# A two-group attention layer: another queue and earlier places for the copies that begin the precomputed weight sums

## The chip, the cores and the metric

The kernel runs on one core of one Trainium2 chip. The metric is the device time of one execution in microseconds (us), the median of several runs. An execution has five engines with a program each: PE (matrix multiply; its weight loads are shown as PEld), DVE, ACT and POOL (elementwise work), and SP, which here only issues DMA transfers. ACT and POOL can issue DMA transfers too. All transfers share the core's 16 DMA engines.

## What is computed

One layer of a hybrid encoder for 1024 new positions ("prompt") and 32 further ones with a cache of 512. After a combined input projection come two attentions, A (top-k sparse, softmax) and B (stick-breaking), two gated branches, and a feed-forward network. Only its end is needed here:

```python
m = jax.nn.sigmoid(gate_a) * pa + jax.nn.sigmoid(gate_b) * pb
h = x + jnp.einsum('bld,de->ble', m, w_out)
u = jnp.einsum('bld,df->blf', rmsnorm(h, g_ffn), w_up)
return h + jnp.einsum('blf,fd->bld', jnp.square(jax.nn.relu(u)), w_down)
```

Sizes: model width 1024, feed-forward width 4096, 8 heads of 64 in each attention, all in float32. The matrix w_up is 1024 x 4096, 16 MB.

## The kernel before

**Tiles and stages.** The 1056 positions are columns. Weights come in units of [128, 512] float32 (256 KB): `unit` loads one from HBM to the tile `wst` (3 buffers), ACT rounds it into `wh` and POOL (sometimes DVE) takes the rest into `wl` (5 buffers each), and each product is then three matmuls (`wh` by `xh`, `wh` by `xl`, `wl` by `xh`). The stages in order of time: indexer and projections of mixer B; top-k and projections of mixer A (line 616, up to about 480 us); the early half of both attentions with gate projections between them (`attend`, lines 635 to 641, about 480 to 700 us); gates, branches and output of group 1, which is columns 0 to 511; the feed-forward network of group 1 (`ffn_group`, about 880 to 1320 us), with the late half of the attentions (the generator `late`, line 634) set between its units up to about 1137 us; then branches, output and feed-forward of group 2, the other 544 columns (`ffn_quads`).

`ffn_group` runs over 8 blocks `q`. A block has four `go_up(f)` (two units of w_up each, 24 matmuls of 128x512) and eight `go_down(e, q)` (one unit of w_down each, 12 matmuls). At the end it reloads 2 MB of `h` (`reload`, tile `xh<-dh`) and scales the output (`late_scale` and others, tile `y`).

**Weight sums.** Group 2 multiplies blocks of w_up with a scheme of seven products instead of eight (Strassen and Winograd). For it four sums of the four blocks w11, w12, w21, w22 are needed for each quarter of w_up: s1 = w21 + w22, s2 = s1 + w11, s3 = w11 + w21, s4 = s2 + w12. The generator `weight_sums` (line 430) makes them in HBM without any compute engine: a plain HBM-to-HBM copy of 1 MB begins a sum (`begin`, issued by SP), and a DMA that adds 1 MB to what is there ends it (`add`, issued by POOL, the only engine here that issues adding DMAs). 4 quarters x 4 sums make 16 copies and 16 adds. Their results, named `dw_up` in the profile, are read from about 1335 us on, as units of group 2.

**What sets the order.** All instructions are recorded by a planner (class `Plan`): `record` notes an instruction with its rank and its dependencies, and a list scheduler picks, engine by engine, the ready instruction of the best rank by a model of costs, in which all transfers go through one pipe (line 407). All are issued from line 410, so every row of the profile shows L410. Ranks run from FAST (0) to SLOW (4); a SLOW instruction goes only where its engine has nothing better that is ready in the model. `behind()` makes instructions depend, in the model only, on the last one recorded before; line 332 applies that to SP's alone. The order that comes out is fixed in the program; on the chip each engine takes its rows one after another and waits at semaphores. A step of `weight_sums` is taken at each `tick()` (line 459). The ticks stand in `ffn_group` at `go_up(f)` for f from 12 on and at `go_down(3, q)` for q from 3 on, 25 places for 24 steps.

**Semaphores of transfers.** The transfers that SP and ACT issue take turns on eight completion counters (DMAHW0 to DMAHW7 in the rows below), those of POOL on eight others (DMASW). A transfer waits until an earlier one on its counter has landed.

Of the kernel before, what the change touches and what calls it, by code (L numbers as in the profile page):

```python
# [14 lines left out]
ALU = mybir.AluOpType  # L15
# [37 lines left out]
FAST, PREP, MAIN, FILL, SLOW = 0, 1, 2, 3, 4  # L53
# [44 lines left out]
PE, DVE, ACT, POOL, SP = range(5)  # L98
# [4 lines left out]
class Plan:  # L103
# [175 lines left out]
    def record(self, eng, fn, op, args, kw):  # L279
        args = list(args)  # L280
        out = kw["out"] if "out" in kw else args[0]
        outs = [out] + ([kw["accum_out"]] if kw.get("accum_out") is not None else [])
        rest = args[1:] if "out" not in kw else args
        ins = [x for x in rest if isinstance(x, bass.AP)]
        ins += [x for k, x in kw.items() if isinstance(x, bass.AP) and k not in ("out", "accum_out")]
        reads = list(ins)
        if op == "copy_predicated":
            reads.append(out)
        n = Node()
        n.id, n.eng, n.call = len(self.nodes), eng, (fn, args, kw)  # L290
        n.key = (self.level[-1], n.id)
        n.occ, n.lat = self.cost(eng, op, out, ins, args[2] if op == "scalar_tensor_tensor" else None, kw)
        n.size = 0
        n.table = TABLE.get(args[2]) if op == "activation" else None
        n.store = op == "dma_start" and out.tensor.name not in self.onchip and self.level[-1] != FAST
        if op == "dma_start":
            n.size = 4
            for s in max((out, ins[0]), key=lambda z: z.size()).shape:
                n.size *= s
        n.lock = eng == POOL or eng == DVE and self.locks(op, out, ins, args)  # L300
        n.row = out.tensor.name if eng == PE and self.level[-1] == FILL else None
        n.wait = self.patience
        n.succ, n.need, n.ready, n.end, n.start = [], 0, 0.0, None, None
        self.nodes.append(n)
        deps = set()
        found = []
        for aps, write in ((reads, False), (outs, True)):
            for ap in aps:
                c = self.cells(ap)
                if c is None:  # L310
                    continue
                m, part, idx = c
                w = m.writer[part, idx]
                if (w < 0).any():
                    deps.update(m.old)
                    n.ready = max(n.ready, m.floor)
                deps.update(np.unique(w).tolist())
                if write:
                    for r, rpart, ridx in m.readers:
                        if rpart.start < part.stop and part.start < rpart.stop and self.meet(idx, ridx, m.writer.shape[1]):  # L320
                            deps.add(r)
                found.append((m, part, idx, write))
        for m, part, idx, write in found:
            if write:
                m.writer[part, idx] = n.id
                if m.writer.shape == (1, 1):
                    m.readers = []
            else:
                m.readers.append((n.id, part, idx))
            if not m.touched or m.touched[-1] != n.id:  # L330
                m.touched.append(n.id)
        if eng == SP and self.hold is not None:
            deps.add(self.hold)
        deps.discard(-1)
        deps.discard(n.id)
        for d in deps:
            d = self.nodes[d]
            if d.end is not None:
                n.ready = max(n.ready, self.after(d, n))
            else:  # L340
                d.succ.append(n)
                n.need += 1
        if not n.need:
            heapq.heappush(self.later[eng], (n.ready, n.id))
# [74 lines left out]
class Layer:  # L419
# [10 lines left out]
    def weight_sums(self):  # L430

        nc, a = self.nc, self.a
        for (w, q), s in self.sums.items():
            w11, w12, w21, w22 = (a[w][i, 4 * q:4 * q + 4].rearrange("t (a b) c -> (t a) (b c)", b=4) for i in range(4))
            s1, s2, s3, s4 = s

            def begin(out, src):
                with nc.behind():
                    nc.sync.dma_start(out, src)

            def add(out, src):
                nc.gpsimd.dma_start(out, src, accum_op=ALU.add, max_dma_last_dim=8192)

            begin(s1, w21)
            begin(s3, w11)
            yield
            add(s1, w22)
            add(s3, w21)
            yield
            begin(s2, s1)  # L450
            yield
            add(s2, w11)
            yield
            begin(s4, s2)
            yield
            add(s4, w12)
            yield

    def tick(self):

        with self.nc.rank(SLOW):
            next(self.steps, None)

    def split(self, h, l, x):
# [66 lines left out]
    def run(self):  # L531
        nc, a = self.nc, self.a
# [82 lines left out]
        self.rope_tables()  # L615
        for p in range(4):
            self.project_a(p)
        with nc.rank(SLOW):
            self.top_k()
        for e in GATES:  # L620
# [13 lines left out]
        late = (None for is_a in (False, True) for h in range(H) for _ in self.attend(h, is_a, (4, 6)))  # L634
        for is_a in (False, True):
            for h in range(H):
                for _ in self.attend(h, is_a, (0, 2)):
                    pass
                for _ in range(AHEAD if is_a and h == H - 2 else 0):
                    next(late)  # L640
                if h in NEWS:
                    self.attend_new(NEWS.index(h), is_a)
# [1019 lines left out]
    def ffn_group(self, g, late=iter(())):  # L1662
        nc, a = self.nc, self.a
        nq, us = DFF // 512, {}

        def source(name, row, col, t):

            return a[name][2 * row + col, t]

        def go_up(f):  # L1670
            units = [self.unit(source("w_up", f % 8 // 4, j, 4 * (f // 8) + f % 4)) for j in range(2)]
            us[f] = uh, ul = g.mh[:, f % 8], g.ml[:, f % 8]

            def done(c, cs, ps):
                r = g.tmp("ru", "pb", 3)
                nc.scalar.activation(r, ps, AF.Relu)
                nc.gpsimd.tensor_mul(r, r, r)
                nc.scalar.copy(uh[:, cs], r)
                nc.vector.tensor_sub(ul[:, cs], r, uh.bitcast(F32)[:, cs])

            self.column_block(units, lambda k, cs: (g.h[:, k, cs], g.l[:, k, cs]), done, g.chunks)

        def go_down(e, q):
            units = [self.unit(source("w_down", e % 2, q % 2, 4 * (q // 2) + e // 2))]

            def done(c, cs, ps):
                y = g.y[:, e, cs]
                if q == 0:
                    nc.scalar.copy(y, ps)
                elif q < nq - 1:  # L1690
                    nc.vector.tensor_add(y, ps, y)
                elif e < KB // 2:
                    self.late_scale(g, e, c, cs, ps)
                else:
                    self.finish(g, e, c, cs, ps)

            if q == nq - 1 and e >= KB // 2:
                for c, cs in enumerate(g.chunks):
                    self.early_scale(g, e, c, cs)
            self.column_block(units, lambda k, cs: (us[4 * q + k][0][:, cs], us[4 * q + k][1][:, cs]), done, g.chunks,  # L1700
                              kn=4)

        done = 0

        def beside(n):

            nonlocal done
            done += n
            while done >= PACE:
                done -= PACE  # L1710
                nc.patience = WAIT[2]
                with nc.behind():
                    next(late, None)
                nc.patience = WAIT[1]

        go_up(0)
        self.scales(g)
        for q in range(nq):
            for f in range(4 * q + 1, min(4 * q + 5, 4 * nq)):
                go_up(f)  # L1720
                if f >= 12:
                    self.tick()
                beside(2)
            if q == nq - 1:
                self.reload(g)
                for e in KEEP:
                    go_down(e, q - 1)
            for e in range(KB):
                if q != nq - 2 or e not in KEEP:
                    go_down(e, q)  # L1730
                if q >= 3 and e == 3:
                    self.tick()
                beside(1)
        for _ in self.steps:
            pass
# [85 lines left out]
```

## Time and profile before

| | |
|---|---|
| time, median of 3 runs | 1782.49 us (1781.36 to 1785.09) |
| the profiled execution's own time | 1796.3 us |
| ACT, busy share of the span | 57% |
| POOL, busy share of the span | 60% |
| DVE, busy share of the span | 65% |
| bytes moved by DMA | 289.71 MB |

The profile is one execution with the hardware profiler on, taken apart from the timed runs. Its span goes from the first instruction to the last; the execution's own time has what lies around it too. PE's busy time counts overlapping matmuls as busy time and their ends are modelled, so a stage is judged here by how many matmuls start in it, too.

### The profile page before, as it was taken

How to read it: one execution, taken by the hardware profiler on the slowest of the kernel's cores; microseconds unless marked ns; L12 is line 12 of the kernel's file. 1: busy time of each engine (PE TensorE's matmuls, PEld its weight loads, DVE VectorE, ACT ScalarE, POOL GpSimd, SP SyncE). 2: the span in 40 equal slices, each digit the busy share in tenths (PEclk: the TensorE clock that was granted, in tenths of full speed). 3: DMA queues.
4: the chain of work that ended last, by engine and by line, in shares of the span. 5: the costliest groups of instructions: out<-in, count | busy, mean ns of one | idle time of the engine just before them, and what ended most of it. 6: DMA issues, size and time to landing. Idle time of an engine off the chain costs nothing.

```text
span 1794.5 us, 32622 instructions
## 1 busy us (share of the span) xinstructions
PE 1740.3 (97%) x11202; PEld 1586.7 (88%) x11202; DVE 1164.0 (65%) x2448; ACT 1015.4 (57%) x2249; POOL 1070.5 (60%) x901
## 2 busy tenths in 40 slices
PE   8999999999999998999999999998999999999998
PEld 7999999999999888988888888886779999999998
DVE  7555678999566544788765546321245877777888
ACT  7344699963256666667665537522225665747472
POOL 4622333335366574999865446664667966656774
PEclk9999999999999999999999999999999999999999
DMA  8244452544666577556344387688885644444453
GB/s 260 70 126 127 120 160 65 161 142 143 192 168 160 157 198 207 162 171 176 107 137 139 101 225 191 204 244 218 233 283 170 188 119 137 129 130 130 136 175 96
DMA packets 168118, 289.71 MB, mean 161 GB/s; under 512 B 28944, under 2 KB 58224, under 8 KB 165648
## 3 DMA queue, kind: packets, MB, share of 16 engines
q1 hardware_dynamic: 165216, 270.50, 50.7%
q0 software_dynamic: 2304, 16.78, 4.9%
q8 instruction: 89, 1.46, 0.4%
q14 instruction: 77, 0.63, 0.1%
q10 hardware_dynamic: 432, 0.34, 0.1%
HBM read 233.04 MB, written 87.96 MB: 179 GB/s over the span
## 4 chain that ended last, share of the span: by engine, by line
PE 78%; DMA 8%; DVE 7%; POOL 2%; issue 2%; ACT 1%; SPq 0%; POOLq 0%; DVEq 0%; ACTq 0%
PE pj L410 53%; PE s L410 13%; PE t L410 5%; PE o L410 4%; DMA wst<-w_up 4%; PE pd L410 2%; POOL wl L410 1%; DMA wst<-w_down 1%; DVE pj L410 1%; DMA q<-dq 1%; DVE xl L410 1%; ACT wh L410 1%; DVE wst L410 0%; DVE raw L410 0%; DMA k<-dk 0%
## 5 line engine op out<-in xcount | busy, mean ns | idle before, releaser
L410 PE MATMUL pj<-xh,wh 128*128 128x512 f32 (+1 forms) x1864 | 640.5, 344 | 15.6 <-ACT wh L410 7.1
L410 POOL TENSOR_TENSOR wl<-wst,wh 128x512 fp32r<-128x512 f32 x324 | 459.8, 1428 | 323.1 <-ACT wh L410 293.5
L410 PE MATMUL pj<-xh,wl 128*128 128x512 f32 (+1 forms) x1864 | 639.7, 344 | 5.2 <-POOL wl L410 5.1
L410 PE MATMUL pj<-xl,wh 128*128 128x512 f32 (+1 forms) x1864 | 636.5, 342 | 0.7 <-DVE xl L410 0.7
L410 PEld LDWEIGHTS pj<-xh,wh 128*128 128x128 f32 x1864 | 354.4, 190 | 54.5 <-ACT wh L410 10.3
L410 PEld LDWEIGHTS pj<-xh,wl 128*128 128x128 f32 x1864 | 353.8, 190 | 42.1 <-POOL wl L410 8.8
L410 PEld LDWEIGHTS pj<-xl,wh 128*128 128x128 f32 x1864 | 354.2, 190 | 34.0 <-DVE xl L410 1.2
L410 ACT CAST wh<-wst 128x512 fp32r<-128x512 f32 x342 | 211.0, 621 | 287.3 <-PE pj L410 123.2
L410 DVE TENSOR_TENSOR tt<-t,tt 128x512 fp32r<-128x512 f32 (+2 forms) x168 | 100.5, 623 | 47.1 <-ACT tt L410 45.3
L410 DVE TENSOR_TENSOR_SCAN rem<-rem 128x896 f32<-128x896 f32 (+6 forms) x66 | 117.6, 1806 | 11.8 <-ACT rem L410 11.4
L410 ACT ACTIVATE junk<-score,cand 128x384 bf16<-128x384 f32 (+1 forms) x124 | 116.0, 936 | 9.5 <-DVE cand L410 7.5
L410 POOL TENSOR_TENSOR p<-p,rem 128x895 f32<-128x895 f32 (+6 forms) x66 | 101.6, 1552 | 29.5 <-DVE rem L410 23.2
L410 DVE TENSOR_TENSOR y<-pj,y 128x512 f32<-128x512 f32 (+1 forms) x95 | 55.5, 584 | 88.7 <-PE pj L410 88.5
L410 PE MATMUL s<-k,q 128*128 128x384 f32 (+5 forms) x384 | 97.4, 359 | 10.2 <-DMA k<-dk 3.3
L410 ACT CAST tt<-t 128x512 fp32r<-128x512 f32 (+2 forms) x168 | 84.9, 540 | 37.8 <-PE t L410 33.1
L410 PEld LDWEIGHTS o<-tt,v 128*128 128x128 f32 x640 | 93.8, 191 | 9.6 <-ACT wh L410 0.8
L410 PE MATMUL s<-wl,xh 128*128 128x256 f32 (+1 forms) x360 | 101.8, 286 | 0.2 <-POOL wl L410 0.2
L410 PE MATMUL s<-wh,xh 128*128 128x256 f32 (+1 forms) x360 | 100.3, 286 | 0.9 <-DVE small L410 0.7
L410 PE MATMUL s<-wh,xl 128*128 128x256 f32 (+1 forms) x360 | 100.8, 283 | 0.0
L410 PE MATMUL o<-tt,v 128*128 128x256 f32 (+1 forms) x640 | 99.6, 279 | 0.4 <-ACT wh L410 0.4
L410 PE MATMUL t<-ident,p 128*128 128x128 f32 x596 | 90.4, 276 | 2.5 <-POOL p L410 2.5
L410 DVE TENSOR_TENSOR xl<-ru,xh 128x512 fp32r<-128x512 f32 x32 | 36.1, 1127 | 84.0 <-ACT xh L410 83.9
(341 smaller groups left out, 3879.0 us busy)
## 6 DMA issues: line engine op xcount, KB each, us to landing
wst<-w_down SPq DMA_DIRECT2D x85, 256.0 KB, 2.8
wst<-w_up SPq DMA_DIRECT2D x80, 256.0 KB, 2.9
q<-dq SPq DMA_DIRECT2D x64, 256.0 KB, 5.2
dw_up<-w_up POOLq DMA_DIRECT2D x16, 1024.0 KB, 10.6
k<-dk SPq DMA_DIRECT2D x48, 256.0 KB, 3.9
v<-dv SPq DMA_DIRECT2D x48, 256.0 KB, 3.8
wst<-w_g SPq DMA_DIRECT2D x42, 256.0 KB, 3.3
dv<-vs SPq DMA_DIRECT2D x32, 256.0 KB, 2.7
```

The source lines that it names most:

```text
L410: fn(*args, **kw)
```

## The change

`weight_sums` now begins all four sums of a quarter with a plain block of w_up (s1 with w21, s3 with w11, s2 with w11, s4 with w12) and adds the rest (w22, w21, s1, s2), so that no copy reads the result of another transfer. ACT issues the copies. Each step is one copy; the add that ends a sum is held back two steps, so 16 steps have a copy each, from the third on also an add, and a 17th step issues the last two adds. `tick` puts each step behind the last recorded instruction (`behind`), and line 332 now applies that to the transfers of any engine. The ticks stand in three places: one after each of the four `project_a`, one at heads 0, 3 and 6 of either early attention (six), and in `ffn_group` at every third `go_up` (f = 3, 6, ... 30).

```diff
-        if eng == SP and self.hold is not None:
+        if op == "dma_start" and self.hold is not None:
             deps.add(self.hold)
...
     def weight_sums(self):
 
         nc, a = self.nc, self.a
+        held = []
+
+        def add(out, src):
+            nc.gpsimd.dma_start(out, src, accum_op=ALU.add, max_dma_last_dim=8192)
+
         for (w, q), s in self.sums.items():
...
-            begin(s1, w21)
-            begin(s3, w11)
+            for out, src, more in ((s1, w21, w22), (s3, w11, w21), (s2, w11, s1), (s4, w12, s2)):
+                nc.scalar.dma_start(out, src)
+                held.append((out, more))
+                if len(held) > 2:
+                    add(*held.pop(0))
+                yield
+        for x in held:
+            add(*x)
             yield
-            add(s1, w22)
-            add(s3, w21)
-            yield
-            begin(s2, s1)
-            yield
-            add(s2, w11)
-            yield
-            begin(s4, s2)
-            yield
-            add(s4, w12)
-            yield
 
     def tick(self):
 
-        with self.nc.rank(SLOW):
+        with self.nc.rank(SLOW), self.nc.behind():
             next(self.steps, None)
...
         for p in range(4):
             self.project_a(p)
+            self.tick()
...
             for h in range(H):
+                if h % 3 == 0:
+                    self.tick()
                 for _ in self.attend(h, is_a, (0, 2)):
...
                 go_up(f)
-                if f >= 12:
+                if f % 3 == 0:
                     self.tick()
                 beside(2)
...
-                if q >= 3 and e == 3:
-                    self.tick()
                 beside(1)
```

The planner orders everything anew, so the effect on the program is seen best in its rows. SP's queue in the last part of `ffn_group`, after the late attentions: `wst<-w_up` and `wst<-w_down` are loads of weight units, `dw_up_NN` the sums. Before:

```order
L410 DMA wst<-w_up 128x512 x7
L410 DMA dw_up_91<-dw_up_90 16x16384
L410 DMA wst<-w_up 128x512
L410 DMA wst<-w_down 128x512 x4
L410 DMA dw_up_94<-w_up 16x16384
L410 DMA dw_up_93<-dw_up_91 16x16384
L410 DMA wst<-w_down 128x512 x2
L410 DMA dw_up_96<-w_up 16x16384
L410 DMA wst<-w_down 128x512 x2
L410 DMA wst<-w_up 128x512 x2
L410 DMA dw_up_95<-dw_up_94 16x16384
L410 DMA wst<-w_up 128x512 x6
```

The same place in the changed program, with the stretch that follows up to the reload of `h`:

```order
L410 DMA wst<-w_up 128x512 x8
L410 DMA wst<-w_down 128x512 x8
L410 DMA wst<-w_up 128x512 x8
L410 DMA wst<-w_down 128x512 x6
L410 DMA wst<-w_up 128x512 x6
L410 DMA wst<-w_down 128x512 x7
L410 DMA xh_108<-dh 128x8x512
```

The copies are gone from SP's queue, and only weight loads are left. POOL's rows at the same place, where `ru` is work of `go_up`; before:

```order
L410 DMA dw_up_94<-w_up 128x2048
L410 DMA dw_up_93<-w_up 128x2048
L410 TENSOR_TENSOR wl<-wst,wh 128x512 x2
L410 DMA dw_up_96<-w_up 128x2048
L410 TENSOR_TENSOR wl<-wst,wh 128x512 x4
L410 DMA dw_up_95<-w_up 128x2048
L410 TENSOR_TENSOR wl<-wst,wh 128x512 x2
```

And in the changed program:

```order
L410 DMA dw_up_99<-dw_up_98 128x2048
L410 TENSOR_TENSOR wl<-wst,wh 128x512 x2
L410 TENSOR_TENSOR ru<-ru 128x512
L410 TENSOR_TENSOR wl<-wst,wh 128x512 x2
L410 TENSOR_TENSOR ru<-ru 128x512
L410 TENSOR_TENSOR wl<-wst,wh 128x512 x2
L410 DMA dw_up_101<-dw_up_99 128x2048
L410 TENSOR_TENSOR wl<-wst,wh 128x512 x8
```

These are the last two adds of the program; before, 12 of the 16 stood from `dw_up_90` on, all in this part. The third place is ACT's queue where the early attentions begin (`p` and `rem` are their weights, `s` their scores), with the semaphores that each row waits for, in the changed program:

```order
L410 CAST wh<-wst 128x512 [waits DMAHW6_49,PE_49,Pool_49]
L410 DMA dw_up_89<-w_up 16x16384 [waits DMAHW2_49]
L410 DMA dw_up_90<-w_up 16x16384 [waits DMAHW4_49]
L410 ACT_TABLE_LOAD [waits DMAHW0_49]
L410 ACTIVATE y_6557<-y_6557 128x512 [waits DVE_49]
L410 ACTIVATE p<-s 128x384 [waits PE_49]
```

Before, ACT's queue had no transfer here. A copy takes its turn on SP's eight counters: DMAHW2 here is that of the transfer which SP issues eight places ahead of the copy in the program. Of the 16 copies 12 have such a wait in their row.

More of the change, by code (lines that the diff above doesn't have):

```diff
@@ L435, in weight_sums @@
             s1, s2, s3, s4 = s
[L437 to L442, printed above, removed]
-            begin(s1, w21)
-            begin(s3, w11)
-            yield
-            add(s1, w22)
-            add(s3, w21)
-            yield
-            begin(s2, s1)
-            yield
-            add(s2, w11)
-            yield
-            begin(s4, s2)
-            yield
-            add(s4, w12)
+            for out, src, more in ((s1, w21, w22), (s3, w11, w21), (s2, w11, s1), (s4, w12, s2)):
[6 more added lines that the diff above has]
+            add(*x)
             yield
     def tick(self):
-        with self.nc.rank(SLOW):
+        with self.nc.rank(SLOW), self.nc.behind():
             next(self.steps, None)
```

## The prediction

> **What bounds the kernel now.** I read the page first, then the stages, then the chain of work in order of time.
>
> ```profile
> span 1794.5 us, 32622 instructions
> PE 1740.3 (97%) x11202; PEld 1586.7 (88%) x11202; DVE 1164.0 (65%) x2448; ACT 1015.4 (57%) x2249; POOL 1070.5 (60%) x901
> PE 78%; DMA 8%; DVE 7%; POOL 2%; issue 2%; ACT 1%; SPq 0%; POOLq 0%; DVEq 0%; ACTq 0%
> ```
>
> PE is the bound as a whole, but the chain spends 8% of the span, over 140 us, in DMA. Only a stage can tell where that costs time. The stages of group 1's feed-forward network (window; PE busy and matmuls begun; PEld, DVE, ACT, POOL; granted clock; DMA share; GB/s):
>
> ```profile
> 895.00:1050.00 155.00, 155.00 (x862) 135.06 (x861) 86.70 (x201) 91.38 (x175) 86.89 (x71) 1.00 0.46 135
> 1050.00:1080.00 30.00, 26.62 (x125) 21.84 (x123) 10.14 (x30) 8.20 (x15) 11.46 (x10) 1.00 0.92 214
> 1080.00:1138.00 58.00, 57.82 (x338) 50.94 (x339) 34.17 (x88) 34.74 (x67) 33.45 (x31) 1.00 0.62 172
> 1138.00:1195.00 57.00, 57.00 (x253) 47.19 (x252) 11.79 (x14) 23.79 (x42) 43.30 (x35) 1.00 0.77 234
> 1195.00:1318.00 123.00, 108.31 (x436) 83.62 (x435) 30.21 (x35) 33.03 (x57) 73.97 (x63) 0.96 0.88 251
> ```
>
> From 1138 on nothing but 128x512 matmuls runs, so their count is a clock: 253 in 57 us is 0.225 us each. From 1195 to 1318 only 436 begin. The chain says why (start, length, what; its first line is the share by cause in this window):
>
> ```profile
> by line: DMA wst<-w_up 34.9%; PE pj L410 19.5%; DMA wst<-w_down 17.2%; POOL wl L410 12.4%; ACT wh L410 5.6%; POOL y L410 5.1%; issue 4.8%; ACT ru L410 0.3%; POOLq L410 0.3%; ACTq L410 0.1%; POOL ru L410 0.1%
> 1137.59 57.23 PE pj L410 x252
> 1214.66 18.45 DMA wst<-w_up
> 1263.81 17.59 DMA wst<-w_up
> 1308.83 4.48 POOL y L410 x4
> ```
>
> The second row gives 57.23 / 252 = 0.227 us a matmul. PE needed 436 x 0.227 = 99.0 us and took 123: **24.0 us are lost**. More than half of the chain there is weight loads, single ones of 18 us. What slows them shows in the transfers from 1198 to 1318 (queue, packets, MB, share of 16 engines; loads with their median time to landing), with the load of a stage without sums, 895 to 1035, as the last row:
>
> ```profile
> q1 hardware_dynamic: 6656, 21.24, 48.3%
> q0 software_dynamic: 1261, 9.15, 39.6%
> wst<-w_down SPq DMA_DIRECT2D x20, 256.0 KB, 6.3
> wst<-w_down SPq DMA_DIRECT2D x16, 256.0 KB, 2.6
> ```
>
> q0 holds POOL's adds: 9.15 MB took 39.6% of 120 us, 47.5 us, **5.2 us of all 16 engines for each MB added**. q1, loads and copies together, took 58 us for 21.24 MB, 2.7 us a MB. With the sums beside it a load lands in 6.3 us, without them in 2.6.
>
> **The change, part by part.** To place the moved steps I counted the `wh` casts ahead of each copy on ACT in the changed program, and the `wl` rows ahead of each add on POOL, and read when the trace of before reaches the same cast. The first copy, the last copy and the last add fall here (start, length):
>
> ```profile
> 354.24 0.60 ACT L410 CAST wh<-wst 128x512 fp32r<-128x512 f32 x1
> 1154.56 0.61 ACT L410 CAST wh<-wst 128x512 fp32r<-128x512 f32 x1
> 1223.22 1.27 POOL L410 TENSOR_TENSOR wl<-wst,wh 128x512 fp32r<-128x512 f32 x1 [6.37 <-ACT wh L410]
> ```
>
> Three copies and one add come before 475, seven copies and seven adds from 475 to 760, six copies and six adds from 890 to 1195, and the last two adds near 1198 and 1223.
>
> *Term A, 1195 to 1318.* Nine adds (9.15 MB) and the nine copies that SP issues here leave; two adds come. DMA then has 2 x 5.2 us for adds and 21.24 - 9 = 12 MB x 2.7 = 33 us for loads, 43 of 123 us, against 0.88 before. A unit feeds 12 matmuls, 2.7 us, and its load lands in 2.6 us with three `wst` and five `wh`/`wl` buffers ahead of PE, so one add at a time is covered. What is late next is the end of the group: the scaling of `y` on POOL (4.48 us above) stands ahead of `wl` rows and waits for the 2 MB reload. Bounds: -24.0 if all goes; -2.5 if POOL's 17.5% of this chain (`wl` and `y`, 21.5 us) is a limit of its own. I keep 4 us of loss, about that `y` row, since one stage earlier the same `wl` work cost nothing. **A = -20.**
>
> *Term B, 1050 to 1080.* 30.0 - 26.62 = 3.4 us are idle after two copies and two adds that were issued within 15 us (the copies' rows stand under C). One copy and one add fall there now. Between 0 and -3.4, I take half, rounded: **B = -2**.
>
> *Term C, the early attentions,* where steps are new. Their loads have little time in hand. PE's waits from 475 to 830, the stage, its transfers, and what one idle gap does to the clock:
>
> ```profile
> PE s L410 <- DMA k<-dk: 3.3, 2, 2.9
> PE s L410 <- DMA q<-dq: 2.5, 2, 2.1
> 475.00:760.00 285.00, 276.10 (x1784) 251.65 (x1783) 162.63 (x341) 174.49 (x392) 183.78 (x163) 0.98 0.65 176
> q1 hardware_dynamic: 37856, 49.84, 64.1%
> 580.00:600.00 20.00, 17.87 (x119) 16.71 (x119) 15.58 (x36) 10.40 (x26) 8.98 (x8) 0.91 0.56 145
> ```
>
> Seven steps add 7 x (5.2 + 2.7) = 55 us of engine time to 285, so the share goes from 0.65 to about 0.84. Upper end: every step holds up a load that PE needs at once by the whole 5.2 us of its add, and the gap costs clock too (0.09 x 20 = 1.8 us in the last row): 7 x 7.0 = 49. Lower end: -3, if some of the 8.9 us that are idle there (285 - 276.1) go in the new order. The nearest rows lie close to zero, SP's copies beside late attentions:
>
> ```profile
> 1036.91 0.56 SPq L410 DMA_DIRECT2D dw_up<-w_up  x1
> 1042.55 0.52 SPq L410 DMA_DIRECT2D dw_up<-w_up  x1
> 1087.45 0.51 SPq L410 DMA_DIRECT2D dw_up<-dw_up  x1
> 1107.40 0.52 SPq L410 DMA_DIRECT2D dw_up<-dw_up  x1
> ```
>
> The last two, each with its add some 8 us behind it, fall in the row 1080 to 1138, which has 0.18 us idle; the first two, with two adds at once, are the burst of term B, 1.7 us a step. Seven steps at 0.1 to 1.7 are 1 to 12. The new order also leaves room: 71 gate matmuls stand between the issue of the first `k` load and the first score, where 32 stood (counted over the program's rows). Between 1 and 12, **C = +5.**
>
> The new queue in itself I cost at nothing. The Trainium skill, "DMA: Bandwidth & Descriptors", section "Issuing engines are not separate DMA queues", says the same: transfers from the scalar, sync and gpsimd queues run on the same 16 engines and interleave, and several issuers save only sequencer time. If the scalar queue brought engines of its own, C would be near 0 and the sum 5 us lower; by the rule it stays. No run here yet shows a copy from that queue.
>
> *Term D, issue time and waits.* Issue times (ns, least/median/most), the landing of the two kinds of copy, and SP's waits for copies and adds:
>
> ```profile
> L410 SPq DMA_DIRECT2D dw_up<-w_up x8: 495/520/1278, 1036.9 to 1262.5; - x8
> L410 POOL DMA_DIRECT2D dw_up<-w_up x16: 725/820/1045, 1046.6 to 1319.9; - x16
> dw_up<-w_up SPq DMA_DIRECT2D x8, 7.3
> SPq L410 <- DMA dw_up<-w_up: 15.1, 4, 4.5
> ```
>
> SP loses 16 issues and the 15.1 us it stood behind adds; that is part of why its loads were late in A, and is not counted again. ACT gains 16 x 0.52 = 8 us, hidden by its idle time (174.49 busy of 285 above). POOL's 16 adds of 0.82 us only move. New is the wait on a shared counter: while ACT waits, casts of `tt` and `wh` and the exponentials stand behind it, and PE waits for those. At the copy near 556, say, the transfer eight places back is a gate's store:
>
> ```profile
> 548.00 0.32 SPq L410 DMA_DIRECT2D dg<-gz  x1
> 555.57 0.59 SPq L410 DMA_DIRECT2D q<-dq  x1
> dg<-gz SPq DMA_DIRECT2D x32, 136.0 KB, 2.6
> ```
>
> It lands at about 550.6, 5 us before ACT comes; by the same count over all ACT rows from 350 to 1200, the transfer eight back had landed over 2 us earlier in 95 of 100. The other way round, SP's eighth transfer behind a copy waits 7.3 us for its landing; SP issues eight in 5 to 12 us there, so it may stand for 2 us. From 0 to 7 x 2 = 14 if PE felt each one; hidden by the buffers, I take **D = +1**.
>
> *Term E.* The new order of all rows may move other waits either way; 0, with 5 us to each side.
>
> **Sum:** -20 - 2 + 5 + 1 = -16. The profiled execution took 1796.3 (1.8 around its span), so it would take 1780.3. The median of the timed runs lies 13.8 below the profiled one, at 1782.5; the same 16 gives **1766.5**. If part of the 13.8 is contention that only the profiler adds, A is smaller in the timed runs; that is one reason to keep the range open upwards.
>
> **The rivals.**
> *Everything is free* (C and D at 0, all 24 of A, 3.4 of B): 1782.5 - 27 = 1755. For it: the row 1080 to 1138. Against: the low slack of `k` and `q`.
> *The loss stays or is given back in equal size* (1780). PE would still lose at 1195 to 1318 because of POOL's `wl` and `y` (17.5% of that chain), or C would eat 16 to 24 us. Against the first: from 1138 to 1195 the same POOL work, 43.30 busy of 57, cost PE nothing.
> *Slower: the early attentions become DMA-bound.* Loads there wait behind adds as weight loads did from 1195 on, at a share of 0.84 against 0.88. With 5.2 us and a clock drop at five to six of seven steps, C is 35 to 40, and the time 1782.5 - 22 + 40 = 1800. It decides from 22 / 7 = 3 us a step. For it: attention loads are needed within a few us. Against: 0.1 to 1.7 us a step beside late attentions.
> *The steps come late after all,* since they are SLOW on a busy ACT and pile up in the feed-forward network: half of A goes, 1776.5. The rows of ACT and POOL speak against it.
>
> **How the numbers follow.** Forecast 0.55 (1766.5, own range 1757 to 1776); everything free 0.17; late steps 0.03; no net change 0.14; slower 0.11. A change of 0.2%, 3.6 us, is about what a measurement of this kernel can tell from none. Faster is 0.55 + 0.17 + 0.03 = 0.75, the same 0.14, slower 0.11. For 8 in 10 the range cuts the fast tail below 1752 and leaves most of the slow rival out above 1788.
>
> **What would show it.** A: in the last 120 us of the feed-forward network `wst` lands in under 3.5 us, some 0.227 us pass per matmul, and the clock is 1.00. B: no idle 3 us near 1050. C: from 475 to 760 PE is idle 10 to 16 us instead of 8.9, with `k` and `q` ahead; 25 or more would make the slower rival true. D: ACT waits under 10 us in all for SP's transfers. If the copies are not on ACT's queue, or the first 128x512 stretch still takes 0.28 us a matmul, the prediction is wrong at its root.

## The result and the profile after

| | time, us | ratio to before, 95% interval |
|---|---|---|
| before | 1782.49, median | 1 |
| after | 1802.55, median (1795.05 to 1809.96) | 1.0109 [1.0075, 1.0143] |
| after, profiled execution | 1802.19, span 1800.4 | |

The change makes the kernel 1.1% slower, about 19 us, and the forecast had 16 us the other way. Two lines of the page of after first:

```profile
span 1800.4 us, 32600 instructions
PE 76%; DVE 9%; DMA 7%; issue 3%; POOL 2%; ACT 2%; SPq 0%; POOLq 0%; ACTq 0%; DVEq 0%
```

The page says little: the chain's share of DMA has gone only from 8% to 7%. The stages say more. The end of group 1's feed-forward network did what the change could be hoped to do. These are windows of after (length; PE busy and matmuls begun; PEld, DVE, ACT, POOL; granted clock; DMA share; GB/s), and one row of its chain of waits (start, length, what):

```profile
1154.50:1211.50 57.00, 57.00 (x268) 47.69 (x267) 18.10 (x23) 26.66 (x47) 41.58 (x33) 1.00 0.57 168
1211.50:1311.50 100.00, 100.00 (x443) 82.78 (x442) 24.57 (x26) 32.82 (x57) 61.65 (x51) 1.00 0.46 125
1166.26 178.77 PE pj L410 x811
```

811 matmuls follow each other without a wait (the last of them are smaller ones of group 2), where before the chain broke off after 252 and then went through loads of weights of up to 18 us. From 1211 on 100 us hold 443 matmuls, 0.226 us each, and the clock is 1.00. The time was lost earlier. PE's waits from 430 to 860 in after (us in total, times, longest), then one row of SP's waits there:

```profile
PE s L410 <- DMA q<-dq: 8.6, 1, 8.6
PE s L410 <- DMA kc<-dk: 6.5, 3, 4.4
PE pj L410 <- ACT xh L410: 4.6, 2, 4.0
SPq L410 <- DMA dg<-gz: 14.9, 2, 11.5
```

Before, PE's largest totals there were 3.3 and 2.5 us. The largest one now has a story, and the chain of after tells it (start, length, what). The first three rows are from the timelines of ACT and POOL:

```profile
480.24 1.14 ACTq L410 DMA_DIRECT2D dw_up<-w_up  x2
483.04 0.84 POOL L410 DMA_DIRECT2D dw_up<-w_up  x1
483.60 1.12 POOL L410 DMA_DIRECT2D dw_up<-dw_up  x1
...
469.99 11.79 PE pj L410 x74
...
482.27 12.64 DMA dg<-gz
...
495.02 0.32 SPq L410
...
496.08 8.58 DMA q<-dq
...
504.71 2.82 PE s L410 x9
```

Two steps fall together at 480: that after the last `project_a` and that at head 0. Two copies and two adds, 4 MB, are issued within 5 us. The small store `dg<-gz`, 136 KB, median 2.6 us before, takes 12.64 us. Two rows behind it on SP stands the load of `v`. It does not read `dg`, but waits for that store's completion counter (the 11.5 above), and the two loads of `q` stand behind it. The counter that `v` itself raises is another one, so this is no taking of turns on a shared counter. The kernel closes the pool of `gz` just before it opens that of `v`, so `v` probably lies where `gz` lay; no run shows that. The second `q` then takes 8.58 us, and PE reaches its first scores at 504.71. What the gap does to the clock (windows of after, the second from within the gap):

```profile
475.00:500.00 25.00, 21.08 (x136) 19.09 (x134) 3.50 (x8) 2.84 (x5) 3.81 (x4) 1.00 0.82 221
500.00:510.00 10.00, 5.29 (x17) 4.62 (x18) 2.92 (x3) 2.30 (x6) 1.04 (x2) 0.50 1.07 262
```

The trace's clock record has 0.50 from 499.8 to 510.0: that is the last 4.9 us of the gap and the 5.3 us behind it. So a wait of 8.6 us costs more than 8.6 us.

This place is not the only one. Further on two steps stand close again, with copies at 618 and 639 and adds at 625 and 641, and the chain of after shows another late store of `gz`, with a wait of SP from 640 to 653:

```profile
640.30 11.71 DMA dg<-gz
...
SPq L410 <- DMA dg<-gz: 3.3, 1, 3.3
```

Here a load of a weight takes its turn on the store's counter, and loads of `vc` and `k` follow behind it.

### The profile page after: what moved, and what is told of

The parts are those of the page before. It is cut to its first block, busy times and chain, and to the rows that moved or that the text cites. A ratio compares the mean times of both kernels' runs of the same rounds, so it can differ in the third digit from the quotient of the medians.

```text
span 1800.4 us, 32600 instructions
## 1 busy us (share of the span) xinstructions
PE 1741.6 (97%) x11202; PEld 1591.6 (88%) x11202; DVE 1164.9 (65%) x2448; ACT 1015.0 (56%) x2247; POOL 1059.6 (59%) x901
## 4 chain that ended last, share of the span: by engine, by line
PE 76%; DVE 9%; DMA 7%; issue 3%; POOL 2%; ACT 2%; SPq 0%; POOLq 0%; ACTq 0%; DVEq 0%
PE pj L410 55%; PE s L410 10%; PE o L410 4%; PE t L410 4%; PE pd L410 2%; DMA dg<-gz 2%; DMA q<-dq 1%; POOL p L410 1%; POOL wl L410 1%; DVE pj L410 1%; DMA vc<-cva 1%; DVE junk L410 1%; DVE xl L410 1%; DVE pre L410 1%; DMA o<-do 1%
## 5 line engine op out<-in xcount | busy, mean ns | idle before, releaser
L410 POOL TENSOR_TENSOR wl<-wst,wh 128x512 fp32r<-128x512 f32 x324 | 448.5, 1389 | 334.0 <-ACT wh L410 292.2
L410 POOL TENSOR_TENSOR p<-p,rem 128x895 f32<-128x895 f32 (+6 forms) x66 | 106.3, 1622 | 63.8 <-DVE rem L410 60.4
```

The source lines that it names most:

```text
L410: fn(*args, **kw)
```

## The experiments

Theories: **1**, the bytes of the sums hold up the loads of the early attentions; **2**, the new order of all instructions does it; **3**, ACT at the shared completion counters. The kernel before was first profiled once more, since its first profile was 13.8 us above the median.

> The kernel before, unchanged, profiled once more. Its first profiled execution took 1796.3 us where the timed runs gave 1782.5. If the 24 us that PE lost between 1195 and 1318 are there in every execution, this profile has some 1780 to 1800 us and 22 to 26 us of loss there. If the loss was larger in the profiled execution than in the timed ones, a profile near 1782 shows 8 to 15 us of loss in the last 120 us of group 1's feed-forward network.

It took 1784.55 us, span 1782.8, near the median; the stages below compare with this profile. At the end of the network, 1187 to 1310 here, 453 matmuls begin in 123 us, so at 0.227 us each 20 us are lost where the first profile lost 24: most of the loss is in this execution too.

### The same order without the bytes

`all_tiny` and `adds_tiny` are the changed kernel with every instruction at its place, but with transfers of 16 columns (copies and adds, or the adds alone); group 2 then reads plain blocks of w_up instead of the sums, so the result is not the layer's. `fake` tells the planner the old size. The edit adds two lines above, so rows of these versions show L412.

```diff
-            nc.gpsimd.dma_start(out, src, accum_op=ALU.add, max_dma_last_dim=8192)
+            self.nc.fake = 1 << 20
+            nc.gpsimd.dma_start(out[:, 0:16], src[:, 0:16], accum_op=ALU.add, max_dma_last_dim=8192)
+            self.nc.fake = 0
```

> The changed kernel with the same order of every row, but each of the 32 transfers of the sums moves 1/128 of its bytes, and group 2 reads plain blocks of w_up instead of the sums (its output is then not the layer's). Theory 1, the transfers' bytes slow the loads of the early attentions: the 30 us of new loss there go, and the time is 1765 to 1775. Theory 2, the new order by itself is worse: the loss stays, 1795 to 1803. Theory 3, ACT stands at the shared completion counters: the waits stay, most of the loss too, above 1790.

> The 16 accumulating transfers move 16 columns instead of 1 MB; the copies keep their size, and every instruction keeps its place in the order of the changed kernel. dw_up is then not the sum it should be. Theory 1a (in a step the accumulating transfer, 5.2 us of all 16 engines for its MB, is what holds the early attentions up, the copy's 2.7 us little): with the bytes of both gone the early attentions took 344.3 us instead of 360.9 and the whole 1766; with the adds gone alone most of that comes back: early attentions 345 to 352, whole 1766 to 1780. Theory 1b (the copy's large packets do it): early attentions 355 to 361, whole 1790 to 1800.

`all_tiny` took 1766.05, ratio 0.9902 [0.9870, 0.9935]; `adds_tiny` 1766.11, ratio 0.9935 [0.9916, 0.9954]. Without the bytes of the adds the slowdown is gone; the copies' bytes then cost nothing that shows. The chain of `adds_tiny` at the place of the story above:

```profile
469.95 26.47 PE pj L412 x161
496.42 1.32 PE s L412 x9
```

Same rows, same two copies, and PE waits for nothing. The store still takes 6.72 us there and SP waits 5.7 for it, so the copies alone stretch it too, but only the adds on top reach PE.

Since the order is the same in both versions, the same row can be looked up in each. DVE's `y` behind the gap and its `o` near the end of the early attentions, in after and in `adds_tiny`:

```profile
511.96 0.69 DVE L410 TENSOR_TENSOR y<-pj,rb 128x512 f32<-128x512 f32 x1 [1.90 <-PE pj L410]
752.58 0.42 DVE L410 TENSOR_TENSOR o<-o 64x256 f32<-64x256 f32 x1 [5.31 <-ACT o L410]
```

```profile
500.96 0.69 DVE L412 TENSOR_TENSOR y<-pj,rb 128x512 f32<-128x512 f32 x1
722.00 0.42 DVE L412 TENSOR_TENSOR o<-o 64x256 f32<-64x256 f32 x1 [0.66 <-ACT o L412]
```

So the doubled step costs 11.0 us, and after is 30.6 us behind by 753. Rows between them put it 18.8 behind at 654 and 23.2 at 710: the loss comes in several places, and the doubled step is a third of it.

The same edit in the kernel before tells what its adds cost:

> The kernel before, every instruction at its place, with the 16 accumulating transfers cut to 16 columns, so that the sums are not made. What is left is the kernel before without the bytes of the adds. By the analysis the adds cost before the lost time at the end of the feed-forward network (A, 20 to 24 us) and near 1050 (B, 3 us): 1755 to 1762; the order of before is then some 5 to 10 us better than that of the changed kernel, 1766 without the adds. Rival (the two orders are equal without bytes, and the whole 20 us of the change is bytes): 1766 and the adds cost before only 16 us.

1759.17 us, ratio 0.9860 [0.9839, 0.9882]: 25 us, by the ratios. The rival of 16 us falls. Now the stages of these kernels can be set against each other. First window: up to SP's first load of a w_up unit; second: to the last `w_bb` load behind the reload of `h`, that is group 1's feed-forward network and its end. In turn before profiled again, before without the adds' bytes, after, after without them:

```profile
0.00:809.00 809.00, 791.89 (x5236) 724.70 (x5237) 571.57 (x1394) 510.07 (x1203) 424.42 (x392) 1.00 0.54 158
809.00:1326.90 517.90, 499.86 (x2566) 420.88 (x2565) 244.58 (x439) 249.16 (x472) 329.30 (x253) 1.00 0.65 186
```

```profile
0.00:810.30 810.30, 792.79 (x5236) 724.91 (x5237) 570.82 (x1394) 510.36 (x1203) 424.03 (x392) 1.00 0.54 157
810.30:1304.40 494.10, 491.79 (x2549) 420.19 (x2548) 242.09 (x438) 249.62 (x472) 330.52 (x254) 1.00 0.52 162
```

```profile
0.00:856.30 856.30, 815.97 (x5298) 742.95 (x5299) 578.73 (x1404) 517.22 (x1223) 430.08 (x403) 0.98 0.59 172
856.30:1341.10 484.80, 480.99 (x2468) 410.26 (x2468) 237.06 (x426) 241.64 (x449) 316.21 (x242) 1.00 0.55 158
```

```profile
0.00:825.90 825.90, 805.48 (x5299) 734.20 (x5299) 580.31 (x1404) 517.04 (x1223) 430.63 (x403) 1.00 0.56 168
825.90:1306.60 480.70, 479.02 (x2468) 409.11 (x2467) 236.93 (x426) 241.36 (x449) 315.77 (x242) 1.00 0.47 142
```

A stage may be compared between a kernel and its own version without bytes, where the order is the same (the counts of matmuls agree, but for some records that are missing). Between two orders it may not: after begins 62 matmuls more ahead of its first w_up load than before. What the bytes of the 16 adds cost, from these rows and the spans (the rest is the span less both windows):

| us | to first w_up load | feed-forward network | rest | whole span |
|---|---|---|---|---|
| before | 809.0 - 810.3 = -1.3 | 517.9 - 494.1 = 23.8 | -0.3 | 1782.8 - 1760.6 = 22.2 |
| after | 856.3 - 825.9 = 30.4 | 484.8 - 480.7 = 4.1 | 1.7 | 1800.4 - 1764.2 = 36.2 |

The change took 19.7 us of the adds' cost out of the feed-forward network and put 31.7 us into the early part. Of the 30.4 there, 815.97 - 805.48 = 10.5 us are more busy time for the same matmuls, at a mean clock of 0.98 instead of 1.00, and the rest is waiting. The order without bytes costs 1764.2 - 1760.6 = 3.6 us by the profiles and 13 by the timed ratios (0.9935 - 0.9860 = 0.0075, with an uncertainty of 0.003). So the 19 us are 6 to 14 us of bytes and 4 to 13 of order; a sharper split the runs don't give. That the cost of bytes moved is not in doubt.

### Without the steps in the early attentions

```diff
-                if h % 3 == 0:
-                    self.tick()
...
-                if f % 3 == 0:
+                if f % 2 == 0:
                     self.tick()
```

> The changed kernel without the six steps beside the early attentions; the 13 remaining ones go at every second go_up instead of every third. Theory 1: the loss in the early attentions falls to that of before (some 12 us with the clock), the end of group 1's network stays free, 1762 to 1775. Theory 2: the order is new again, so nothing is sure, 1775 to 1800. Theory 3: as theory 1.

1770.90 us, ratio 0.9928 [0.9894, 0.9963]: **faster than both kernels**, with the sums complete. With its adds' bytes taken away:

> The faster version without steps in the early attentions, every instruction at its place, its 16 accumulating transfers cut to 16 columns. If it is faster because its adds stand where loads have time in hand, their bytes cost it 5 to 12 us: 1759 to 1766. If its order is better by luck and its bytes cost as much as elsewhere (25 us or more): below 1746.

1761.72, ratio 0.9879 [0.9861, 0.9898]. The two in the same windows, with the bytes and without:

```profile
0.00:814.40 814.40, 794.38 (x5238) 724.11 (x5239) 572.10 (x1395) 506.35 (x1202) 420.52 (x394) 1.00 0.56 165
814.40:1309.90 495.50, 489.66 (x2529) 417.08 (x2528) 247.17 (x435) 248.79 (x469) 329.45 (x252) 1.00 0.63 181
```

```profile
0.00:812.60 812.60, 794.89 (x5238) 725.32 (x5239) 573.43 (x1395) 506.33 (x1202) 420.00 (x394) 1.00 0.55 162
812.60:1299.80 487.20, 487.04 (x2529) 416.23 (x2528) 246.22 (x435) 248.71 (x469) 328.42 (x252) 1.00 0.51 154
```

Two of its adds stand in the early part and 14 in the feed-forward network. Their bytes cost 1.8 us early and 8.3 in the network, 8.4 over the span (1768.3 - 1759.9). Without the bytes this order is as good as that of before, 1759.9 against 1760.6. What makes this version fast is where its adds stand.

### The doubled step, the queue, the packets

The step at head 0 of the first attention is left out, so that the two at 480 don't meet:

```diff
-                if h % 3 == 0:
+                if h % 3 == 0 and (is_a or h):
                     self.tick()
```

> The changed kernel without the step at the first early attention, which put two copies and two adds within 4 us at 480; every later step moves by one place. In the profile PE then stood 8.8 us and ran 10 us at half clock, 14 us together. Theory 1: those 14 us go, 1785 to 1792. Theory 2: no change, 1798 to 1806. Theory 3: no change beyond 3 us.

1790.02, ratio 1.0031 [1.0011, 1.0052], as expected: 14 us of the 19 by the ratios, for one step of seven. Every later step moves by a place here, so the order is another one; by the rows of the same order above the doubled step cost 11.0.

The copies issued from SP, at the steps of the changed kernel (the planner's order differs):

```diff
-                nc.scalar.dma_start(out, src)
+                nc.sync.dma_start(out, src)
```

> The changed kernel with its copies issued from SP instead of ACT, at the same steps. Theory 1 (bytes in the early attentions): the queue is worth little, the early attentions stay at 350 to 365 us, whole 1793 to 1808. Theory 3b (copies on ScalarE's queue share completion counters with SP's loads, and that is what turns a late store into a late q load): early attentions below 345 us, whole 1780 to 1788. If SP standing behind the sums matters: over 1810.

1797.03, ratio 1.0102 [1.0070, 1.0134], the same as after within the intervals. Its profiled execution, 1788.72, was the fastest of its five; PE's waits from 430 to 860 lead with the same load:

```profile
PE s L410 <- DMA q<-dq: 7.7, 1, 7.7
PE pj L410 <- ACT xh L410: 3.7, 1, 3.7
```

The queue shows no gain or loss, within some 8 us, and theory 3 falls: without copies on ACT the time is the same.

The adds cut into packets of 2 KB, in the changed kernel's order:

```diff
-            nc.gpsimd.dma_start(out, src, accum_op=ALU.add, max_dma_last_dim=8192)
+            nc.gpsimd.dma_start(out, src, accum_op=ALU.add, max_dma_last_dim=2048)
```

> The changed kernel with the accumulating transfers cut into packets of 2 KB instead of 8 KB; the order of all engines' instructions is the changed kernel's. Theory P (a small load waits behind whole 8 KB packets of the accumulation on each engine, so shorter packets let it through): early attentions 340 to 352 us, whole 1775 to 1790. Theory 1 in bytes (the engines are taken for the time that the bytes need, whatever the packets): 358 to 364 us, whole 1795 to 1808. Third way (each short packet has a cost of its own): slower than 1810.

1803.20, ratio 1.0107 [1.0077, 1.0137]. The adds' queue from 430 to 860 (packets, MB, share of 16 engines), in after and here:

```profile
q0 software_dynamic: 1152, 8.39, 10.4%
```

```profile
q0 software_dynamic: 4224, 8.39, 11.1%
```

With 3.7 times the packets the engines' time is nearly the same (0.104 x 430 = 45 us, 5.3 us for each MB) and so is the time of the kernel. It goes by bytes, not by packets.

### Other places for the steps

`ffn_steps_only`: new queue and plain blocks, but the steps only at `go_up` from f = 12 on.

```diff
             self.project_a(p)
-            self.tick()
...
-                if h % 3 == 0:
-                    self.tick()
...
-                if f % 3 == 0:
+                if f >= 12:
                     self.tick()
```

> The changed kernel, copies on ScalarE's queue and plain blocks as there, but with its steps only where go_up of the last feed-forward tiles stood before (f from 12 on), none at mixer A's projections or between the early attentions. Theory 1 (the spreading is the only part of the change that moves time: it frees the end of the feed-forward network and crowds the early attentions): back to about the kernel before, 1775 to 1795, with weight loads late again at the end of the feed-forward network and the early attentions at 324 to 330 us. Rival (queue and plain blocks carry a gain of their own, since SP no longer stands behind the sums): 1760 to 1772.

1815.65, ratio 1.0213 [1.0193, 1.0232]: a miss, 20 us above the range. POOL's adds in one stretch, and the longest load of a weight in the chain:

```profile
1213.61 0.82 POOL L410 DMA_DIRECT2D dw_up<-dw_up  x1
1215.31 0.97 POOL L410 DMA_DIRECT2D dw_up<-w_up  x1
1220.74 0.82 POOL L410 DMA_DIRECT2D dw_up<-w_up  x1
```

```profile
1087.07 19.48 DMA wst<-w_down
```

All 16 adds stand from 1084 to 1320, in clusters like this one. The early part is as short as before, 807.2 us, and the feed-forward network takes 548.8 instead of 517.9. So no gain of the new queue and the plain blocks by themselves shows; the clusters could hide one. That clusters of three make the difference to before fits the rows, but was not tested alone.

`early_steps` and `single_early_steps` put steps at the projections, where loads seemed to have time in hand:

```diff
             self.index_projection(1, s)
+            if s % 3 == 2:
+                self.tick()
...
             self.project_b(p)
+            self.tick()
...
             self.gate(e, "zb")
+            self.tick()
...
-                if h % 3 == 0:
-                    self.tick()
```

> The steps are taken out of the early attentions and put at the index projections, after each projection of mixers A and B and each gate ahead of 475 us, where a load has more time in hand; the rest at every third go_up of the feed-forward network. Theory 1: the early attentions lose no bytes to the sums (325 to 335 us), the projections lose at most 1 us a step, the feed-forward network stays as free as in the changed kernel: 1758 to 1770. Theory 2 (the order is what counts, wherever the bytes are): no better than 1775. Rival: the projections are bound by transfers too, and each step costs them 3 us or more: 1780 to 1800.

1798.47, ratio 1.0107 [1.0092, 1.0122]: a miss. Two windows of it, the waits of PE from 270 to 330, and one of DVE there:

```profile
280.00:300.00 20.00, 14.18 (x117) 13.97 (x115) 11.64 (x43) 13.08 (x28) 2.44 (x5) 0.95 0.92 249
300.00:320.00 20.00, 9.54 (x40) 8.54 (x41) 17.77 (x58) 18.06 (x37) 2.31 (x3) 0.67 0.49 154
```

```profile
PE pj L410 <- ACT wh L410: 10.8, 1, 10.8
PE s L410 <- DVE small L410: 5.5, 1, 5.5
DVE gz L410 <- DMA dg<-gz: 6.0, 1, 6.0
```

At 276 two adds and two copies meet again, and PE has 16 us of waits and a clock of 0.67 behind them. A store of `gz` is late here too: DVE stands 6.0 us for its buffer. `single_early_steps` has one step after the last index projection, three at mixer B's projections and four at mixer A's, none at the gates, the rest at every third `go_up`:

> No step between the early attentions. One step each after the last index projection, after three projections of mixer B and after the four of mixer A, none doubled; the other ten at every third go_up. Theory 1c (an added MB is nearly free where it is alone, some 40 us from the next, and costs 10 us or more where two steps come together, as at 276 us of early_steps): projections within 4 us of the kernel before, early attentions 325 to 335 us, feed-forward network as free as in the changed kernel, whole 1757 to 1768. Rival (any step at the projections costs 3 us): 1775 to 1790.

> The version with single early steps, every instruction at its place, its 16 accumulating transfers cut to 16 columns. If its single adds at the projections and in the feed-forward network are nearly free and its order is what makes it 1788: 1775 to 1785. If the bytes of its adds still cost 1 to 1.5 us each, 15 to 25 us in all: 1763 to 1773. Below 1760 the adds cost as much as in the changed kernel, spread or not.

1788.05, ratio 1.0031 [1.0016, 1.0046], and without the adds' bytes 1761.75, ratio 0.9897 [0.9878, 0.9917]. Another miss: the order is as good as any (span 1760.4), and the bytes cost 1786.3 - 1760.4 = 25.9 us although no two steps meet early on. In the windows the cost is spread: 13.8 us for the six adds up to the first w_up load (825.9 - 812.1), 14.2 for the other ten. So an added MB that stands alone isn't nearly free, as I thought after `early_steps`; here 16 of them cost 1.6 us each. Why the same network holds 14 adds for 8.3 us in the fastest version and ten for 14.2 here stays open.

Last, the planner was told that the sums' transfers are a few KB, so that it leaves no room for them, with all bytes moved:

> The changed kernel, all bytes moved, but the planner that sets the order counts each of the sums' transfers as a few KB, so it leaves no room for them. Theory 2b (the changed kernel's order loses its 10 to 12 us in the early attentions because the planner makes room for transfers it takes to be long): PE's waits for other engines near 730 to 765 us go, early attentions 345 to 352 us, whole 1785 to 1793. Theory 2c (the order merely fell differently, room or no room): no systematic gain, 1795 to 1815, and as the loads are issued without regard for the sums, q and k are waited for at least as long.

1823.13, ratio 1.0224 [1.0196, 1.0252], slower than either theory had it. PE's waits from 430 to 860:

```profile
PE s L412 <- DMA q<-dq: 15.2, 3, 14.0
PE s L412 <- DMA kc<-dk: 12.8, 3, 6.3
PE s L412 <- DMA k<-dk: 4.6, 1, 4.6
```

The room that the planner makes for the transfers is no loss: without it `q` and `kc` are waited for nearly twice as long as in after.

## Why the prediction was wrong

**Terms A and B were right.** Forecast -22 together; the adds' bytes cost the feed-forward network 23.8 us before and 4.1 after, 19.7 less. The stretch of 128x512 matmuls runs at 0.226 us each, the clock is 1.00, and the `y` row that was to keep 4 us of loss does not appear in the chain.

**Term C is the step that failed,** and by its size. It had bounds of -3 and 49 and took +5, "0.1 to 1.7 us a step" from adds that stand beside late attentions. The runs show 31.7 us. The engine time was priced rightly (5.2 us an MB, 5.3 measured). In the window that the prediction named PE is idle 285 - 261.75 = 23.3 us, where 8.9 were idle before and 10 to 16 were forecast, with 145 matmuls fewer begun:

```profile
475.00:760.00 285.00, 261.75 (x1639) 236.36 (x1637) 133.37 (x313) 149.40 (x340) 156.52 (x158) 0.95 0.77 209
```

The DMA share is 0.77, below the 0.84 that was expected. The price per step was taken from the wrong rows. Beside the late attentions a step is cheap in after too, where eight adds from 924 on cost 4.1 us, 0.5 each. In the early part eight adds cost 30.4, 3.8 each, because there a late load is needed at once, SP's next loads queue behind a store that is late, and the clock is halved at the end of the gap and behind it. The prediction's own rows pointed there: `k` and `q` already led PE's waits. Its second error in C: two of the seven steps fall together at 480, and it did not price that, though ACT's rows shown with the change have `dw_up_89` and `dw_up_90` next to each other. The rows of the same order put that at 11.0 us, a third of C; `no_double_step`, with an order of its own, puts it at 14.

**The rival "slower"** had 1800, from C of 35 to 40 and a mark of 3 us a step. It is the case that came nearest: loads wait behind adds, and the clock drops, as it said. But that its 1800 is so near the 1802.55 is in part luck. C was 31.7 and not 40, and 5.6 us of order and rest that it did not have make up for most of that. The loss is not even over the steps, a third of it comes from the doubled one, and its own mark, 25 us idle or more, was just missed with 23.3. A chance of 0.11 was too low for a cost whose bounds were 50 us apart.

**Term D was right in the part that it feared.** ACT has no wait of its own queue in the chain (ACTq 0%). The other direction it priced by a copy on the counter; what held SP 11.5 us was a stretched store that the load of `v` depends on, and only the 3.3 us before 652 are a turn on a shared counter. That is a way in which C's bytes act, and it goes with them. That the new queue brings no engines of its own held as well: by the rule of the Trainium skill, "DMA: Bandwidth & Descriptors", section "Issuing engines are not separate DMA queues", and `copies_from_sp` agrees, 1.0102 against 1.0109.

**Term E** was 0 with 5 us to each side; the orders without bytes differ by 3.6 us in the profiles and 13 in the timed runs, so by the timed runs the 5 were too few. The sum with the measured terms of the profiles: -19.7 + 31.7 + 2.0 (rest) + 3.6 = 17.6, which is 1800.4 - 1782.8.

## What to carry to other kernels

Moving a background transfer out of a stage where it costs time only pays if the stage that receives it has loads with time in hand; price it by the waits of that stage, not by its free DMA share, and not by a stage that looks alike. Run the new order once with the transfers cut to a few bytes, and compare by stage: that separates what the bytes cost from what the order costs, which no single profile does. Look in the new order for two such transfers side by side before anything else.

## What the hardware showed

- An accumulating transfer takes 5.3 us of all 16 engines for each MB (45 us for 8.39 MB) in 1152 packets, and 5.7 in 4224. The Trainium skill, "DMA: Bandwidth & Descriptors", section "Queues, rings and completion order", says that an engine takes turns between its queues by whole packets. By that, shorter packets should let small loads pass sooner; the kernel's time stayed at 1803.2 against 1802.55. Whether the packets that the profile counts are those of the rule no run here shows.
- With two copies and two adds under way, a store of 136 KB took 12.64 us; with the copies alone 6.72; the median before was 2.6.
- Gaps of PE cost twice. Around the end of the wait of 8.6 us the granted clock is 0.50, from 499.8 to 510.0 us, and 10.5 of the 30.4 us that the bytes cost the early part of after are longer busy time of the same matmuls. The Trainium skill, "TensorE: Matmul & The Clock Gate", part 1, says that a window of about 3.4 us with an idle PE halves its clock, and that the clock gate has two states, half and full. The 0.50 agrees. The clock records of after and `adds_tiny` hold 1.00 and 0.50 and nothing between, and the stretches at 0.50 last 3.4 us or a multiple of it (6.8, 10.2), but for the one that the span's end cuts; up to 856 us after spends 34 us at 0.50, `adds_tiny` up to 826 us 3.4.
